# Overlapping 8 x 8 windows: from channel groups on a partition to an image's band of rows on a partition

## Chip, cores and metric

One core of one Trainium2 chip. The metric is the device time of one execution in microseconds (us), median of several. The profiled span is 1.7 to 3.2 us shorter than that time. Some executions are called slow because they lie over 1.5% above the fastest of their kernel. Ratios use fast runs alone; where a median or a trace takes in a slow run, or the state is unknown, the text says so.

## The reference

```python
batch, c, h, w = (16, 64, 64, 64)          # float32, window_size 8, stride 4
n_h = n_w = 15
for i in range(n_h):
    for j in range(n_w):
        result[:, i, j] = x[:, :, 4*i:4*i+8, 4*j:4*j+8]     # result: 16, 15, 15, 64, 8, 8
```

It is pure data movement: 16.8 MB in, 59.0 MB out. In HBM one window of one image, all channels, is one run (a contiguous piece) of 64 x 8 x 8 x 4 bytes = 16 KB.

## The kernel before

A partition holds 8 channels of one image. Each window is copied together by VectorE, and leaves by one DMA of 128 runs of 2 KB.

```python
    CHI = P // B                # 8
    CLO = C // CHI              # 8
    gpool = ctx.enter_context(tc.tile_pool(name="gpool", bufs=28))
    L = lpool.tile([P, CLO, H, W], f32)
    x_v = x.rearrange("b (ch cl) h w -> b ch cl h w", ch=CHI)
    nc.sync.dma_start(out=L[:, :, 0:HHALF, :], in_=x_v[:, :, :, 0:HHALF, :])
    nc.sync.dma_start(out=L[:, :, HHALF:H, :], in_=x_v[:, :, :, HHALF:H, :])
    ...
            g = gpool.tile([P, CLO, WS, WS], f32, name="g")
            nc.vector.tensor_copy(out=g[:, :, :, :], in_=src)
            trig[k % 2].dma_start(out=out[:, i, j, :, :, :], in_=g[:, :, :, :])
```

## Time and profile before

| | before |
|---|---|
| time, us | 220.9 (220.69 to 220.94 in the first 3 runs) |
| profiled span, us | 217.7 |
| VectorE busy | 88.7 us, 41% |
| DMA rate, load alone / stores alone | 425 / 354 GB/s |
| end of the load | 46.6 us |

How to read the views: the row "DMA" gives the mean busy share of the 16 DMA engines in 40 slices, in tenths; below it stand the GB/s of each slice. A queue's line gives packets, MB, and the time of its packets as a share of 16 engines' span. A window line gives the stretch, its length, the busy time of each engine, the TensorE clock, the DMA share and GB/s. The lines themselves are in the prediction.

### The profile page before, as it was taken

The page shows a single profiled execution, that of the slowest core. Times are in us where ns is not written, and L with a number is a line of the kernel's source. Part 1 is how long each engine was busy: PE and PEld are TensorE (multiplying, and loading weights), DVE is VectorE, ACT ScalarE, POOL GpSimd, SP SyncE. Part 2 cuts the span into 40 slices and gives each one's busy share as a digit, 9 for nine tenths or more (in the row PEclk, how much of TensorE's full clock was granted, in tenths as well). Part 3 has the DMA queues.
Part 4 walks back from the last instruction along what each step waited for, and adds up shares of the span by engine and source line. Part 5 has one row for each costly group of instructions (what it writes and reads, how often), then busy time and mean ns, then how long its engine had stood idle before and what let it go on. Part 6 is the DMA issues. An engine that isn't in the chain of part 4 may idle for free.

```text
span 217.7 us, 824 instructions
## 1 busy us (share of the span) xinstructions
DVE 88.7 (41%) x225; POOL 0.2 (0%) x4
## 2 busy tenths in 40 slices
DVE  0000691124532446454565555555554554550000
POOL 0000000000000000000000000000000000000000
DMA  6999999989995999999999999999999999999997
GB/s 200 431 425 422 422 423 429 416 311 318 339 345 166 287 321 356 349 353 361 353 358 362 364 354 354 358 355 365 345 341 334 363 363 347 349 343 337 329 338 252
DMA packets 34487, 75.83 MB, mean 348 GB/s; under 512 B 3632, under 2 KB 3632, under 8 KB 32432
## 3 DMA queue, kind: packets, MB, share of 16 engines
q1 hardware_dynamic: 18352, 46.41, 59.0%
q10 hardware_dynamic: 16128, 29.37, 39.2%
q14 instruction: 7, 0.06, 0.1%
HBM read 16.78 MB, written 58.98 MB: 348 GB/s over the span
## 4 chain that ended last, share of the span: by engine, by line
DMA 82%; DVE 7%; issue 1%; DVEq 0%; ACTq 0%
DMA out_dram<-g 72%; DMA L<-in_x_dram 10%; DVE g L50 7%; DVEq L50 0%; ACTq L51 0%
## 5 line engine op out<-in xcount | busy, mean ns | idle before, releaser
L50 DVE COPY g<-L 128x512 f32<-128x512 f32 x225 | 88.7, 424 | 108.0 <-DMA out_dram<-g 83.4
L69 POOL MEMSET const-bfloat16-1.0<- 128x1 bf16 x1 | 0.1, 102 | 0.0
L69 POOL MEMSET const-uint8-127<- 128x1 uint8 x1 | 0.1, 102 | 0.0
L69 POOL MEMSET const-float32-1.0<- 128x1 f32 x1 | 0.1, 99 | 0.0
L69 POOL MEMSET const-float32-0.0<- 128x1 f32 x1 | 0.1, 98 | 0.2 <-issue 0.2
## 6 DMA issues: line engine op xcount, KB each, us to landing
out_dram<-g SPq DMA_DIRECT2D x113, 256.0 KB, 5.5
out_dram<-g ACTq DMA_DIRECT2D x112, 256.0 KB, 5.2
L<-in_x_dram SPq DMA_DIRECT2D x2, 8192.0 KB, 33.9
```

The source lines that it names most:

```text
L50: nc.vector.tensor_copy(out=g[:, :, :, :], in_=src)
L69: nc = _bacc.Bacc("TRN2", target_bir_lowering=False, num_devices=1)
```

## The change

A partition is now an image's band of 8 rows, with all 64 channels, p = 8 x image + band. For even window rows i = 0, 2, ..., 14 a partition has everything it needs, and one DMA per column j stores 128 runs of 16 KB. For odd window rows the lower half comes from the next partition by a stream shuffle, and 7 DMAs of 16 partitions (p = q, q + 8, ...) store 16 runs of 16 KB each. The intent is longer runs: 16 KB instead of 2 KB for the stores. The price is a load in runs of 2 KB instead of 8 KB.

```diff
-    gpool = ctx.enter_context(tc.tile_pool(name="gpool", bufs=28))
+    gpool = ctx.enter_context(tc.tile_pool(name="gpool", bufs=4))
-    nc.sync.dma_start(out=L[:, :, 0:HHALF, :], in_=x_v[:, :, :, 0:HHALF, :])
-    nc.sync.dma_start(out=L[:, :, HHALF:H, :], in_=x_v[:, :, :, HHALF:H, :])
+    L = lpool.tile([P, C, RB, W], f32)
+    x_v = x.rearrange("b c (hg r) w -> b hg c (r w)", hg=HG)
+    for c in range(C):
+        queues[c % 2].dma_start(out=L[:, c, :, :], in_=x_v[:, :, c, :])
 ...
+    nxt = [min(p + 1, 31) for p in range(32)]
+    o_v = out.rearrange("b i j c r w -> b i j (c r w)")
+    for j in range(NW):
+        cols = slice(j * ST, j * ST + WS)
+        g = gpool.tile([P, C, WS, WS], f32, name="g")
+        chunks = NCH if j == 0 else 1              # 4 pieces for the first column
+        for k in range(chunks):
+            nc.vector.tensor_copy(out=g[:, cs, :, :], in_=L[:, cs, :, cols])
+            nc.sync.dma_start(
+                out=o_v[:, 0:NH:NSLOT, j, k * FREE // chunks : (k + 1) * FREE // chunks],
+                in_=g[:, cs, :, :],
+            )
+        h = gpool.tile([P, C, WS, WS], f32, name="g")
+        nc.vector.tensor_copy(out=h[:, :, 0:ST, :], in_=L[:, :, ST:RB, cols])
+        nc.vector.stream_shuffle(out=h[:, :, ST:WS, :], in_=L[:, :, 0:ST, cols], mask=nxt)
+        for q in range(HG - 1):
+            nc.scalar.dma_start(out=o_v[:, NSLOT * q + 1, j, :], in_=h[q::HG, :, :, :])
```

The lines that set `cs`, the channels of piece `k`, are left out.

More of the change, by code (lines that the diff above doesn't have):

```diff
@@ L28 @@
     f32 = mybir.dt.float32
-    CHI = P // B
-    CLO = C // CHI
-    assert CHI * B == P and CLO * CHI == C
-    lpool = ctx.enter_context(tc.tile_pool(name="lpool", bufs=1))
-    gpool = ctx.enter_context(tc.tile_pool(name="gpool", bufs=28))
-    L = lpool.tile([P, CLO, H, W], f32)
-    HHALF = H // 2
-    x_v = x.rearrange("b (ch cl) h w -> b ch cl h w", ch=CHI)
-    nc.sync.dma_start(out=L[:, :, 0:HHALF, :], in_=x_v[:, :, :, 0:HHALF, :])
-    nc.sync.dma_start(out=L[:, :, HHALF:H, :], in_=x_v[:, :, :, HHALF:H, :])
@@ L44 @@
-    trig = [nc.sync, nc.scalar]
-    k = 0
-    for i in range(NH):
-        for j in range(NW):
-            g = gpool.tile([P, CLO, WS, WS], f32, name="g")
-            src = L[:, :, i * ST : i * ST + WS, j * ST : j * ST + WS]
-            nc.vector.tensor_copy(out=g[:, :, :, :], in_=src)
-            trig[k % 2].dma_start(out=out[:, i, j, :, :, :], in_=g[:, :, :, :])
-            k += 1
+    HG = P // B
+    RB = H // HG
+    assert HG * B == P and RB == 2 * ST and WS == 2 * ST
+    NSLOT = RB // ST
@@ new lines @@
+    FREE = C * WS * WS
+    lpool = ctx.enter_context(tc.tile_pool(name="lpool", bufs=1))
+    gpool = ctx.enter_context(tc.tile_pool(name="gpool", bufs=4))
+    L = lpool.tile([P, C, RB, W], f32)
+    x_v = x.rearrange("b c (hg r) w -> b hg c (r w)", hg=HG)
+    queues = [nc.sync, nc.scalar]
+    for c in range(C):
+        queues[c % 2].dma_start(out=L[:, c, :, :], in_=x_v[:, :, c, :])
+    NCH = 4
+    CC = C // NCH
+    nxt = [min(p + 1, 31) for p in range(32)]
+    o_v = out.rearrange("b i j c r w -> b i j (c r w)")
@@ new lines @@
+    for j in range(NW):
+        cols = slice(j * ST, j * ST + WS)
+        g = gpool.tile([P, C, WS, WS], f32, name="g")
+        chunks = NCH if j == 0 else 1
+        cw = C // chunks
+        for k in range(chunks):
+            cs = slice(k * cw, (k + 1) * cw)
+            nc.vector.tensor_copy(out=g[:, cs, :, :], in_=L[:, cs, :, cols])
[8 more added lines that the diff above has]
+            nc.scalar.dma_start(out=o_v[:, NSLOT * q + 1, j, :], in_=h[q::HG, :, :, :])
```

## The prediction

> **What bounds the kernel now.** I read the page first, then the DMA view in three stretches, because only transfers seemed to matter. The page:
>
> ```profile
> DVE 88.7 (41%) x225; POOL 0.2 (0%) x4
> ...
> DMA  6999999989995999999999999999999999999997
> GB/s 200 431 425 422 422 423 429 416 311 318 339 345 166 287 321 356 349 353 361 353 358 362 364 354 354 358 355 365 345 341 334 363 363 347 349 343 337 329 338 252
> DMA packets 34487, 75.83 MB, mean 348 GB/s; under 512 B 3632, under 2 KB 3632, under 8 KB 32432
> ...
> q1 hardware_dynamic: 18352, 46.41, 59.0%
> q10 hardware_dynamic: 16128, 29.37, 39.2%
> ...
> DMA out_dram<-g 72%; DMA L<-in_x_dram 10%; DVE g L50 7%; DVEq L50 0%; ACTq L51 0%
> ```
>
> The 16 DMA engines are busy in nearly every slice, the two queues' shares add to 98%, and 82% of the chain that ended last is DMA. VectorE works 41% of the span. So the kernel is bound by DMA engine time, and the question is only how many nanoseconds of engine time each byte costs. The packet counts give the sizes: 225 stores x 128 = 28,800 packets of 2 KB, 2 loads x 1,024 = 2,048 packets of 8 KB, and 227 x 16 = 3,632 completion packets below 512 B. The DMA view of three stretches (load alone, load beside stores, stores alone) gives the costs:
>
> ```profile
> DMA packets 949, 7.64 MB, mean 425 GB/s; under 512 B 16, under 2 KB 16, under 8 KB 16
> ...
> q1 hardware_dynamic: 949, 7.64, 101.1%
> ...
> q1 hardware_dynamic: 873, 7.15, 84.6%
> q10 hardware_dynamic: 711, 1.31, 17.0%
> ...
> DMA packets 20594, 37.52 MB, mean 354 GB/s; under 512 B 2289, under 2 KB 2289, under 8 KB 20590
> ...
> q1 hardware_dynamic: 10310, 18.77, 52.0%
> q10 hardware_dynamic: 10280, 18.72, 51.1%
> ```
>
> Load alone (5 to 23 us): 1.011 x 16 x 18 us = 291 us over 933 packets of 8 KB, 312 ns each. Load beside stores (25 to 45 us): 0.170 x 16 x 20 us = 54.4 us over 711 - 71 = 640 packets of 2 KB, 85 ns each. Stores alone (84 to 190 us): 0.511 x 16 x 106 us = 867 us over some 9,140 packets of 2 KB, 95 ns each. The single packet records agree: nearly all 8 KB packets take exactly 309 ns, four in five of the 2 KB packets exactly 84 ns, a completion packet 9 ns. Through 84 and 309 goes a line of 75 ns per 2 KB plus about 9 ns per packet. What lifts the mean of the stores from 84 to 95 ns is a tail[...]: 11 ns x 8 packets = about 85 ns per store DMA and engine. With 8 KB load packets in between (the second stretch) this tail is absent.
>
> So an engine pays for 16 KB of store now 8 x 84 + 9 + 85 = 766 ns, and 225 such units make 172 us; the load 2,048 x 312 / 16 = 40 us. There are also holes: the slice marked 5 moved 166 GB/s, about 3 us lost there, when both issuing queues waited for landings.
>
> [...]
>
> **The change part by part.**
> *Load.* 2 DMAs of 8 KB runs become 64 DMAs of 128 x 2 KB, 32 on each queue. Per engine 64 x (8 x 84 + 9) = 43.6 us, plus between 0 and 64 x 85 ns = 5.4 us of completion tail (into SBUF, and other packets can hide it; I take 2). With about 2 us before the first packet flows, the load ends near 48 us. It is all on the path: instead of stores under its second half, there is only the j = 0 chunk work at its very end. Issue does not bind: a DMA issue took 0.54 to 0.8 us when not held up, 32 on each queue is about 21 us.
> *VectorE.* 225 copies of 0.43 us go. [...] 3.93 MB of stores that need 9.3 us at 424 GB/s. It lies beside the stores, except for h of j = 0 at the start.
> *Stores.* The bytes stay: 225 units of 16 KB per engine. As one packet a unit costs 8 x 75 + 9 = 609 ns, so 137 us. Completion packets: 18 + 105 = 123 x 9 ns = 1 us. Completion tail: the even stores pay once in 8 units, 18 x 85 ns = 1.5 us; the odd ones end after every unit, 105 x 85 ns = 9 us if never hidden. Both queues alternate, and the next packet of the other queue lasts 600 ns, so as in the second stretch most is hidden; I count 2 us in all. Stores 140 us against 172.
> *Buffers and semaphores.* Four buffers of 16 KB give two of each kind. The instruction order shows that DMAs share eight completion semaphores, and an issue waits until the earlier DMA on its semaphore has landed. In the steady state one even store (2 MB) and up to seven odd stores (1.8 MB) are in flight. [...] I expect no holes there.
> *Ends.* Switch from load to stores 1.5 us, last landing and end 2 us.
> Sum: 48 + 140 + 3.5 = 191.5 us span. The time before is 220.9 for a profiled span of 217.7; with the same 3.2 us it is 195.
>
> **The rivals.**
> (1) [...] Against it: in before no 8 KB load packet was slowed beyond the start-up. That proves nothing for 16 partitions. A middle outcome is 205 to 225.
> (2) HBM writes as such limit at 354 GB/s, whatever the packet: the stores stay at 167 to 172 us and the time is 220 to 226, for the load becomes dearer by 4 to 8 us and loses its overlap. Against it: most packets take 84 ns even in stores alone, which is 390 GB/s over 16 engines[...].
> (3) The tail is paid fully on every odd store and load: 195 + 8 + 3 = about 206.
> (4) VectorE becomes the bound[...]. Then 200 to 230[...].
>
> **Range and chances.** The plain sum gives 195. All rivals lie above; below is only the case in which more overlaps than I count (no tail, earlier start of stores under the load's end: 188). I put (2) at 8%, a strong (1) or (4) at 12%, a weak (1) or (3) at 25%. So the point is 196, the range 187 to 218. Faster by over 2% means below 216.5.
>
> **What would show it.** Right: 16 KB packets near 609 ns, stores at 415 to 425 GB/s in a stretch of stores alone; 2 KB load packets near 84 ns and the load's end at 46 to 50 us; DMA busy 9 in all slices; [...]. Wrong: 16 KB packets of 800 to 1200 ns[...]; zeros in the DMA row between columns (the semaphores or two buffers each are too few); VectorE without idle time (rival 4); a load past 55 us (2 KB loads cost more than the 2 KB stores tell).

The sum: load 48, stores 140, ends 3.5, so 191.5 us of span and 195 of time. Its 2 us before the first packet, the 2 and 2 us of tail and the 1.5 and 2 us at the ends are estimates; in the trace of before the first packet starts at 2.2 us, and the last store packet ends 1.2 us before the span does. Of the 8 KB packets two thirds took exactly 309 ns, and from 5 us on none took over 321. Every DMA left 16 completion packets (3,632 for 227 before, 2,992 for 187 after). Eight semaphores take the landings, before and after, and the SP queue of before waited 80.1 us for landings at its store issues. The times of the new vector instructions, which the trace of before does not hold, made the 89 us of VectorE, beside the stores and so not in the sum. The trace after has them: 2.28 us for a copy of 4,096 elements, 1.23 for 2,048, 0.69 for 1,024, 2.41 for a shuffle, 86.5 in all.

## The result, and the profile after

374.5 us (373.34 to 376.1, 4 runs) against 220.9: slower by 69% (ratio 1.694, interval 1.687 to 1.701). All ratios here are the mean time of one kernel's fast runs over that of the other's of the same rounds, so not quite the ratio of the medians. The result is correct. The prediction, 196 with a range of 187 to 218, was wrong by a wide margin and in the wrong direction.

The page of the changed kernel:

```profile
span 371.6 us, 393 instructions
...
DVE 86.5 (23%) x63; POOL 0.2 (0%) x4
...
DMA  7999999899489999795894958949599495738797
GB/s 213 282 283 284 284 282 331 214 233 258 134 194 229 284 224 295 198 222 130 169 217 109 222 129 171 233 104 212 127 194 215 99 220 118 183 71 187 180 233 191
...
q1 hardware_dynamic: 7200, 39.85, 44.4%
q10 hardware_dynamic: 7968, 35.92, 39.4%
...
L66 DVE COPY g<-L 128x2048 f32<-128x2048 f32 x15 | 18.4, 1226 | 196.3 <-DMA out_dram<-g 196.3
```

Three things stand out. First, in the slices marked 9 the engines are busy but move only some 280 GB/s while they load and mostly some 225 while they store: a busy engine delivers much less. Second, later slices drop to 4 or 5 at a regular beat, so there are holes as well. Third, VectorE is as busy as predicted (86.5 us; shuffles of 2.41 us) but one group, the first half of the odd tile (L66), waited 196 us for stores. The timeline of one column shows the beat:

```profile
220.04 1.23 DVE L66 COPY g<-L 128x2048 f32<-128x2048 f32 x1 [17.30 <-DMA out_dram<-g]
221.19 0.01 DVE L67 LOAD_MASK_SELECT g<-L  x1
221.19 2.41 DVE L67 STREAM_SHUFFLE g<-L 128x2048 f32<-128x2048 f32 x1
223.49 2.28 DVE L59 COPY g<-L 128x4096 f32<-128x4096 f32 x1
...
225.80 23.59 SPq L60 DMA_DIRECT2D out_dram<-g  x2
243.06 1.23 DVE L66 COPY g<-L 128x2048 f32<-128x2048 f32 x1 [17.29 <-DMA out_dram<-g]
```

A column takes 243.06 - 220.04 = 23.0 us; 9.3 had been expected. The even store issued at 225.8 lands 17.2 us later, and at that very moment the next odd copy starts.

The buffers say why. The trace has no addresses; these are from a build of the changed kernel (A to D stand for the four):

```
column      0    1    2    3    4    5    6    7   ...
even tile   A    C    A    A    D    B    C    A
odd tile    D    B    C    A    D    B    C    A
```

From column 3 on, the odd tile gets the buffer that the even tile *of the same column* is about to leave. So its copy has to wait for the whole 2 MB even store. The pool did not rotate. The waits of the trace agree with the table.

### The profile page after: what moved, and what is told of

Read it like the earlier page. It is cut to its first block, busy times and chain, and to the rows that moved or that the text cites. A ratio compares the mean times of both kernels' runs of the same rounds, so it can differ in the third digit from the quotient of the medians.

```text
span 371.6 us, 393 instructions
## 1 busy us (share of the span) xinstructions
DVE 86.5 (23%) x63; POOL 0.2 (0%) x4
## 2 busy tenths in 40 slices
DMA packets 15170, 75.79 MB, mean 204 GB/s; under 512 B 2992, under 2 KB 2992, under 8 KB 11696
## 4 chain that ended last, share of the span: by engine, by line
DMA 57%; ACTq 21%; DVE 11%; issue 4%; SPq 1%; DVEq 0%
DMA out_dram<-g 41%; ACTq L69 21%; DMA L<-in_x_dram 16%; DVE g L67 8%; DVE g L59 3%; DVE g L66 1%; SPq L44 1%; DVEq L59 0%; DVEq L66 0%
## 5 line engine op out<-in xcount | busy, mean ns | idle before, releaser
L66 DVE COPY g<-L 128x2048 f32<-128x2048 f32 x15 | 18.4, 1226 | 196.3 <-DMA out_dram<-g 196.3
L59 DVE COPY g<-L 128x4096 f32<-128x4096 f32 (+1 forms) x18 | 34.7, 1926 | 67.3 <-DMA L<-in_x_dram 60.9
L67 DVE STREAM_SHUFFLE g<-L 128x2048 f32<-128x2048 f32 x15 | 36.1, 2406 | 0.0
## 6 DMA issues: line engine op xcount, KB each, us to landing
out_dram<-g SPq DMA_DIRECT2D x14, 2048.0 KB, 17.2
```

The costliest lines, as they stand in the source:

```text
L59: nc.vector.tensor_copy(out=g[:, cs, :, :], in_=L[:, cs, :, cols])
L66: nc.vector.tensor_copy(out=h[:, :, 0:ST, :], in_=L[:, :, ST:RB, cols])
L67: nc.vector.stream_shuffle(out=h[:, :, ST:WS, :], in_=L[:, :, 0:ST, cols], mask=nxt)
```

## The experiments

Eleven kernels ran. The theories at the start: **S** (the odd tile waits for the even tile's buffer), **P** (which partitions a DMA reads sets the time of its packets), **W** (16 KB runs are slow to write as such), and several for the load. No run shows by what mechanism partitions or addresses slow a packet. Packet durations quoted as medians or means come from the trace's single packet records.

**Two pools.** Even and odd tiles get two buffers each from a pool of their own.

```diff
-    gpool = ctx.enter_context(tc.tile_pool(name="gpool", bufs=4))
+    gpool = ctx.enter_context(tc.tile_pool(name="gpool", bufs=2))
+    hpool = ctx.enter_context(tc.tile_pool(name="hpool", bufs=2))
-        h = gpool.tile([P, C, WS, WS], f32, name="g")
+        h = hpool.tile([P, C, WS, WS], f32, name="h")
```

> The changed kernel with two pools of two buffers (one for even, one for odd tiles) in place of one pool of four. Theory S (in the one pool the odd tile of a column takes the very buffer that the even tile of that column has just left, so its copy waits some 17 us for the even store to land): the wait of the odd copy on out<-g falls from 196 us to under 60, and the holes of 4 to 5 us in each column close. If S and [...] both hold, columns take about 3.93 MB / 227 GB/s = 17.3 us instead of 23, and the time is 295 to 315. If the slow packets are only a consequence of the restarts in lockstep, packets fall to 0.65 us and the time to 210 to 230. If S is not a cause, 365 to 376.

The first cut is P, with 16 KB packets of 1.23 us where 0.61 had been forecast; in the trace after, half of the 16 KB packets took 1.20 to 1.30 us. Correct, 288.6 us (286.04 to 290.92, the highest of the four a slow run), 1.303 of before; that is a little under the 295 to 315 that S and P together had forecast. The waits of VectorE, in total, times, longest:

```profile
DVE g L60 <- DMA out_dram<-g: 68.4, 12, 11.8
...
DVE h L67 <- DMA out_dram<-h: 54.3, 11, 12.2
```

The wait of the odd copy falls from 196.3 to 54.3 us, and the odd tile waits for odd stores now. S is a cause, worth 374.5 - 288.6 = 86 us with what came along with it. One caution: the build also ordered the vector instructions anew (from the fourth column on, the even copies stand ahead of the odd ones), so the two kinds of store now run one after the other. From 105 to 170 us 97% of the bytes were even stores, at 304 GB/s; from 195 to 280 us the odd stores ran alone, at 242. The packets stayed slow, 1.01 us in the odd stretch. So S is not all.

**Store shapes by themselves** (wrong result). Stores alone, from one tile, in seven phases with a barrier between them.

```python
    sixteen(28, lambda n: h[n % 7 :: 8, :])                  # 1 step 8, start 0..6 in turn
    sixteen(28, lambda n: h[0::8, :])                        # 2 step 8, start 0
    sixteen(14, lambda n: h[0:16, :])                        # 3 neighbours
    sixteen(28, lambda n: h[n % 7 : n % 7 + 106 : 7, :])     # 4 step 7
    all128(range(0, 4), 1)     # 5 16 KB runs, 2 MB each
    all128(range(4, 8), 4)     # 6 4 KB runs
    all128(range(8, 12), 8)    # 7 2 KB runs
```

> Wrong result on purpose: stores alone, in seven phases with a memset as barrier between them, all from one tile. Theory P[...]: 16 partitions a step of 8 apart, start always 0: 1.2 us a packet, 215 to 230 GB/s; the same with start 0 to 6 in turn: between 220 and 330; 16 neighbouring partitions: 2.4 us, 105 to 115 GB/s; a step of 7: most packets 0.61 us, 330 to 420 GB/s. All 128 partitions with 16 KB, 4 KB and 2 KB runs: 16 KB as low as 227[...], 2 KB about 350. Theory W (writes of 16 KB runs to HBM are slow as such): all four phases of 16 partitions alike, 215 to 230 GB/s, and 16 KB runs of 128 partitions the same. Theory of the prediction: all 400 or more except 2 KB.

One stretch of each phase, in order; the last number is GB/s (one run, so state unknown; the differences are factors, not per cents):

```profile
10.00:32.00 22.00, 0.00 (x0) 0.00 (x0) 1.00 1.00 273
45.00:72.00 27.00, 0.00 (x0) 0.00 (x0) 1.00 0.99 202
90.00:115.00 25.00, 0.00 (x0) 0.00 (x0) 1.00 1.02 105
126.00:142.00 16.00, 0.00 (x0) 0.00 (x0) 1.00 0.99 352
155.00:178.00 23.00, 0.00 (x0) 0.00 (x0) 1.00 1.00 337
188.00:206.00 18.00, 0.00 (x0) 0.00 (x0) 1.00 1.01 373
218.00:238.00 20.00, 0.00 (x0) 0.00 (x0) 1.00 1.03 352
```

Phases 2, 3 and 4 have DMAs of the same size, runs and HBM pattern (phase 3 half as many); only the partitions differ: a step of 8, neighbours, a step of 7. The median packet took 1,275, 2,535 and 613 ns (phase 4 has a slow quarter, so its mean is 725). That is 2, 4 and 1 times 0.61 us, up to some 4%. So which 16 partitions a DMA reads sets its packet time, as P says; why is not shown. Phase 2, at 202 GB/s, is a little below the 215 to 230 expected. The DMA share is 1 in all of them, so a busy engine says nothing of how fast its packets go. W falls: the same 16 KB run takes 613 ns in phase 4. The even store's shape (phase 5) is in between, 780 ns in the mean: it starts slow (188 GB/s in the first 2.9 us of its stretch) and gets faster after a few us.

**Load shapes by themselves** (wrong result), each phase behind a barrier.

> Wrong result on purpose: loads alone in six phases with a memset as barrier. 1 is the load of the change (283 GB/s in the changed kernel). Theory L1[...]: phase 3, pitch 63 x 16 KB, 380 or more, phase 1 and 2 about 283. Theory L2 (2 KB runs cost about 120 ns to read whatever the pattern): phases 1 to 4 all 275 to 295, phase 5 (4 KB runs) 330 to 370, phase 6 (8 KB runs) 410 to 425. Theory L3 (two queues disturb each other): phase 2 faster than phase 1 by over 10%. Theory L4[...]: phase 4, whose SBUF side is the same as phase 1's, equal to phase 1, phase 6 slow as well.

Phases 1 (as the change), 2 (one queue), 3 (other image pitch), 4 (channel layout, 2 KB runs) and 6 (channel layout, 8 KB runs):

```profile
4.00:30.00 26.00, 0.00 (x0) 0.00 (x0) 1.00 1.07 269
38.00:64.00 26.00, 0.00 (x0) 0.00 (x0) 1.00 1.04 264
72.00:100.00 28.00, 0.00 (x0) 0.00 (x0) 1.00 1.06 268
108.00:124.00 16.00, 0.00 (x0) 0.00 (x0) 1.00 1.05 390
...
156.00:170.00 14.00, 0.00 (x0) 0.00 (x0) 1.00 1.00 423
```

The image pitch (L1) and the two queues (L3) do nothing here. 2 KB runs as such (L2) are fine at 390 GB/s: over the whole phase a packet takes 89 ns there and 127 in phase 1. L4 as I had put it falls too, for the SBUF side of phases 1 and 4 is the same 128 partitions. What differs is the HBM side.

**The kernel before with a load in 2 KB runs**, 64 DMAs on two queues, otherwise unchanged.

```diff
-    nc.sync.dma_start(out=L[:, :, 0:HHALF, :], in_=x_v[:, :, :, 0:HHALF, :])
-    nc.sync.dma_start(out=L[:, :, HHALF:H, :], in_=x_v[:, :, :, HHALF:H, :])
+    n = 0
+    for r in range(0, H, 8):
+        for cl in range(CLO):
+            [nc.sync, nc.scalar][n % 2].dma_start(out=L[:, cl, r : r + 8, :], in_=x_v[:, :, cl, r : r + 8, :])
+            n += 1
```

> The kernel before with its load cut into 64 DMAs of 128 x 2 KB on two queues. L2: the load ends at about 60 us instead of 46.6, but part of that was stores beside the load: the time goes up by 8 to 18 us, to 229 to 239. L1 or any cause in the band layout's addresses: packets stay at 84 ns, the time within 2% of before.

Correct, 215.6 us (215.06 to 216.86), ratio 0.976 (interval 0.970 to 0.981): better than before, which neither theory had said, though whether by the 2% that a verdict asks for is unclear, as the interval crosses 0.980. The load runs at 388 GB/s. The first copy starts at 8.7 us instead of 23.5, and the hole of the 13th slice is gone. So cutting the load finely does not hurt; the band layout's addresses do. It is also the fastest correct kernel.

**One dim or two on the HBM side** (wrong result). The band layout addresses HBM as 16 images x 8 bands, two steps that can't be merged into one. The channel layout's 128 runs in the load phase lie at one even step. Theory **D**: two dims on the HBM side make a DMA of 128 partitions slow, one dim does not. Theory **N**: neighbouring short runs of HBM are slow to read.

> Wrong result on purpose: loads, then stores, in six phases with a barrier between. Loads of 128 runs of 2 KB: 1 as the change (two dims on the HBM side, 16 x 8, which can't be merged into one; 265 GB/s in the earlier run), 2 two dims but runs 112 KB apart, 3 one dim, runs touching. Theory D[...]: phase 2 slow, 255 to 300, phase 3 fast, 375 to 395. Theory N (the slow thing is reading neighbouring 2 KB runs of HBM from one engine): phase 2 fast, phase 3 slow. Stores: 4 one dim 2 KB, 5 one dim 16 KB, 6 two dims 16 KB (as the even stores). D: phase 4 above 352 (the two-dim 2 KB phase of the earlier run), near 385, with few packets over 84 ns; phase 5 has packets of 0.61 us from its start and 400 to 425 GB/s, phase 6 starts with packets of 1.2 us. N says nothing on stores: 5 like 6.

The six phases in order:

```profile
9.00:36.00 27.00, 0.00 (x0) 0.00 (x0) 1.00 1.06 270
44.00:66.00 22.00, 0.00 (x0) 0.00 (x0) 1.00 1.06 273
74.00:90.00 16.00, 0.00 (x0) 0.00 (x0) 1.00 1.05 387
98.00:110.00 12.00, 0.00 (x0) 0.00 (x0) 1.00 1.03 378
116.00:131.00 15.00, 0.00 (x0) 0.00 (x0) 1.00 1.03 437
137.00:162.00 25.00, 0.00 (x0) 0.00 (x0) 1.00 0.96 322
```

Every phase falls on the side that D says (phase 5 even above its 400 to 425), and N falls: two dims with runs far apart are slow (273), one dim with touching runs is fast (387). With two dims and touching runs (270), and one dim with runs 128 KB apart (390, phase 4 of the load kernel), all four combinations are measured. For the stores, one dim gives 437 GB/s with 16 KB packets of 611 to 658 ns from the start; two dims give packets of some 1,220 ns in the first microseconds, and 322 GB/s. That the number of dims decides is shown for the loads; the two store phases also differ in where their runs lie in HBM. How the dims do it is not shown: the records do not name the engine that took a packet. One thing stays open: the same 16 x 8 split costs 2 KB loads much (270 against 387 GB/s) and 2 KB stores little (352, phase 7 of the store kernel, against 378). D alone does not say why. The issue of a one-dim load DMA took 0.33 us, that of a two-dim one 0.54 (medians, in the one-dim load run below and in the changed kernel).

**Three attempts with other sizes and orders of the stores**, all with two pools and all correct. (a) Even stores in 4 pieces in every column (`chunks = NCH`):

> Two pools, and every even store in four pieces with runs of 4 KB, as the change does for its first column. If 16 KB runs of the even stores are what costs, 240 to 260. Theory P with the odd stores as the bound (27.5 MB at 242 GB/s when alone, as the end of the two-pool run shows): 270 to 290, no gain worth naming.

268.5 us (fast runs 265.23 to 268.56; the trace is of a slow one, 269.62), a little better than the range of P: even stores rose to 333 GB/s (from 100 to 160 us, 89% of the bytes theirs), while the odd ones alone stayed at 246. (b) Odd stores in the order q = 0, 4, 1, 5, 2, 6, 3 (`for q in (0, 4, 1, 5, 2, 6, 3)`):

> Two pools, and the seven odd stores of a column issued in the order q = 0, 4, 1, 5, 2, 6, 3[...]. [...] the stretch with odd stores alone rises from 242 to 320 to 400 GB/s, the time falls to 240 to 265. [...]: 284 to 292.

277.3 us, a miss by either forecast (the second, 284 to 292, was for an order that does not help): the odd stretch rose only from 242 to 274 GB/s. (c) Even stores too as DMAs of 16 partitions in that order:

> As the last, and the even stores too as eight DMAs of 16 partitions in that order instead of one of 128. [...] stores at 340 to 410 GB/s throughout, time 215 to 245, of which some 63 us is the slow load. If the order does not help: 290 to 320.

256.8 us (fast runs 254.87 to 258.1; the trace is of a slow one, 259.14), again short of what I expected; stores at 306 GB/s. The order matters (274 against 242 GB/s for the odd stores), but changing it does not by itself bring the full rate.

**Taking the two dims away** (wrong result). The two-pool kernel with the same bytes, runs and vector work, but each DMA with one even step on the HBM side, and all output written once. First the load alone:

```diff
-        queues[c % 2].dma_start(out=L[:, c, :, :], in_=x_v[:, :, c, :])
+        queues[c % 2].dma_start(out=L[:, c, :, :], in_=x_f[128 * c : 128 * c + 128, :])
```

> Wrong result on purpose: the two-pool kernel with only its loads changed to one dim. The load ends near 46 instead of 63 us, the stores stay as in the two-pool kernel: 288 minus 15 to 20, so 268 to 274. [...]

273.0 us, so 15.5 us less, as expected. Then all DMAs, with the odd tile as one DMA of 112 partitions:

> Wrong result on purpose: the two-pool kernel with the same bytes, the same runs (2 KB loads, 16 KB stores) and the same vector work, but every DMA addresses HBM with one dim of 128 (odd stores: 112) evenly spaced runs instead of 16 x 8. Every output row is written once. [...] the load ends at 44 to 48 us, 16 KB packets take 0.61 to 0.65 us, and the time is its sum, 190 to 200. If something else holds the kernel back (semaphores, two buffers of a kind, VectorE), 205 to 250 with holes in the DMA row.

The first forecast there is for the case that slow packets and the buffers are all that was wrong with the prediction; "its sum" is the prediction's. 247.8 us (243.65 to 256.25; only the lowest of the four counts as fast, the traced one does not, and there is no ratio). The mean 16 KB packet still took 767 ns, and the DMA share was 0.91. The suspicion: the 112 runs of the odd store make its packets slow. The last run changes only that, 128 runs of 14 KB instead of 112 of 16 KB:

```diff
-            out=o_f[1920 + j : 1920 + j + 15 * 111 + 1 : 15, :], in_=h[0:112, :, :, :]
+            out=o_odd[j : j + 15 * 127 + 1 : 15, :], in_=h[:, 0 : C * 7 // 8, :, :]
```

> Wrong result on purpose: as the last one-dim run, but the odd store too is 128 runs (of 14 KB, the same bytes) instead of 112 of 16 KB[...]. [...] packets go to 0.61 to 0.65 us (16 KB) and 0.54 to 0.58 us (14 KB), and the time to the sum of the prediction, 190 to 202. If two buffers of a kind and whole-tile stores are too few[...], it stays at 225 to 250 with the DMA row below 9.

189.25 us (189.16 to 189.36), ratio 0.854 (interval 0.848 to 0.860). Its page:

```profile
DMA  6999999999889999999999999999999999999996
GB/s 224 335 395 386 388 388 386 386 389 396 357 345 441 413 441 426 448 413 427 413 427 420 426 444 422 432 423 419 420 419 445 429 431 424 426 416 427 423 435 276
...
q1 hardware_dynamic: 7200, 39.85, 52.1%
q10 hardware_dynamic: 6768, 35.92, 46.9%
```

Packets of 16 KB took 618 ns in the mean, of 14 KB 541, of 2 KB 89. There are no holes left, with two buffers of each kind and nothing changed about the semaphores. The output is wrong: this HBM pattern does not fit the band layout, and I found no correct kernel with it.

## Why the prediction was wrong, point by point

- **What bounds before**: right that it is DMA engine time. Wrong in one reading: I took the tail of the 2 KB stores for the price of a completion. In the one-dim 2 KB stores each DMA ends with a completion too, yet only 1% of the packets take over 110 ns (mean 88): there is no such price. In the two-dim 2 KB stores, those of the kernel before among them, 12 to 14% do (mean 94 to 96). So it goes with the two dims; why is not shown.
- **Stores, 16 KB at 609 ns**: the step that failed most. The number is right where every DMA has 128 runs at one even step in HBM (618 in the last run), and a stretch of stores alone then moved 426 GB/s, so rival 2, a limit on writes at 354, falls too. In the changed kernel the packets took 1.14 us (even) and 1.08 us (odd). I had this as rival 1, for the odd stores only; I did not see that the even stores and the load would be slowed too, gave its strong form (with rival 4) 12%, and put its worst at 265; packets of 800 to 1,200 ns stood among my signs of being wrong. My argument against it was that packets would not stay slow. That was the fault: they partly get faster in the back-to-back phase of even stores (337 GB/s), but hardly do in the changed kernel, where each store waits for the one before (in the column from 226 to 243 us three quarters of the packets took over 1.2 us).
- **Load, 84 ns and an end near 48 us**: measured 121 ns and 62.9 us. The 2 KB size was judged nearly right (89 ns with one dim, 84 expected); the two dims were the cause.
- **Buffers, "two of each kind"**: false. I took four buffers for a rotation, where the pool handed the odd tile the buffer of its own column's even tile. No rival had this. It made the holes that I had ruled out.
- **VectorE, 89 us**: right (86.5). The measured times stand beside the prediction.
- **Semaphores and issue do not bind**: right for the last run, but that has one odd store a column and so does not test the seven. In the changed kernel 21% of the chain that ended last is the issue of odd stores (ACTq L69), and in the odd stretch of the two-pool kernel nearly all of it (97% from 239 to 255 us, most issues 0.6 to 1.25 us, where the shortest of that run took 0.5). The store kernel shows that such an issue grows with the time of the packets: in its phases 2, 3 and 4, where only the partitions differ, the first issues took 0.35 to 0.55 us and the median one 2.4, 4.6 and 1.3 us. Still, the odd stores as such went faster on two queues (273 GB/s in phase 1) than here on one (242), so a part may be the single queue; no run tests that in the kernel.

The account, in this order of removal: buffers 374.5 to 288.6 (86 us), two dims in the load 288.6 to 273.0 (16), two dims and few partitions in the stores 273.0 to 189.3 (84); by what mechanism the last two slow the packets is not shown. The last step also makes one odd DMA of seven and lets the build keep the columns in order, so its 84 us are not the dims and partitions alone; the run with 112 partitions has both and still took 247.8, so these two are not enough: going from 112 to 128 runs is worth the other 59 us. What remains, 189.3, is 6 us under the sum of the prediction, 195.

## What to carry to other kernels

Here longer runs paid only where every DMA had 128 runs at one even step in HBM (189.3 us, with a wrong output, against 220.9). So look at which partitions a DMA reads and at the dims of its HBM side, and try such a DMA first. A DMA row full of 9s is no proof of full rate: compare the mean time of a packet with the best one of the same size (here medians of 613 to 2,535 ns for 16 KB, all at a share of about 1). And do not assume that a pool rotates: look at which buffer a tile gets and which store it waits for.
